# Eight gate dots on VectorE stated at other places of the first layer, and more of its sums pinned behind a product

## The chip, the core and the metric

The kernel runs on one core of a Trainium2 chip. The metric is the device time of one execution in microseconds; the time of a kernel is the median of its runs. An execution's time is a little longer than its span, which reaches from the first to the last instruction that the profiler recorded.

## The reference

Two layers over 256 tokens of width 2048, in f32. The first layer is a Mamba-2 mixer: one big input projection gives z, x, B, C and dt; x, B and C go through a causal convolution of width 4 and SiLU; then a state-space sum within one chunk of 256 tokens, in 8 groups of 8 heads; then a gate by SiLU(z), an RMS norm by group, and an output projection. The second layer is a dilated window attention. Each layer is wrapped in an adaptive norm: three vectors (shift, scale and gate) are products of SiLU(c) with a large matrix.

```python
def _adaln(c, w, b):
    mod = jax.nn.silu(c) @ w + b
    shift, scale, gate = jnp.split(mod, 3, axis=-1)
...
        h = x * (1.0 + scale) + shift
...
        x = _layer_norm(DEEPNORM_ALPHA * x + (1.0 + gate) * y, ln_g[layer], ln_b[layer])
```

The first layer's gate is needed only at the end of that layer. Its 2048 entries come from 16 dots, one for every 128 channels; the first eight of them are what the change moves.

The state-space sum of one group, as the kernel does it (one chunk, so the carried state drops out):

```python
        cb = jnp.einsum("blgn,bsgn->blsg", cc, bc)
        y_diag = jnp.einsum("blsgk,bsgkp->blgkp", cb[..., None] * decay, xc)
```

## The kernel before

**Weights in pieces.** All projections stream f32 weights from HBM in pieces of 128x1024 (tile raw, six buffers, loaded on SP's queue by load_piece, line 88). Each piece is split in two halves for the f32r matmuls: ScalarE copies the high half (whi, line 100) and VectorE makes the low half (wlo = raw - whi, line 102). There are four buffers of each half, so a half can be made while PE is up to four pieces behind it. A product then takes three matmuls for each pair of tiles: high by high, high by low, low by high. Lines 155 to 157 are the B and C products ("bc") and the second group's x product, lines 195 and 198 the other x products (cm_wide), and lines 238 to 240 the z products (tm_chunk, through tm_mults). A function called first_or takes a piece that begin_next has already split during the last piece of the product before.

**Order within an engine.** Each engine works through its own queue in order. That order is fixed when the program is built: a scheduler goes through the program and gives an engine, at each point, the oldest stated instruction that is ready by then, so that a younger one can be pulled in front of an older one that is not ready. `tc.issue_after(ins)` adds one fixed edge: what is stated in its block comes behind `ins` in the queue of their engine. It adds no other wait. In the texts, a pin is such an edge.

**The gate dots.** ada_load (line 315) loads one 1 MB slice of the modulation matrix into a tile araw (two buffers, SP's queue, line 317). ada_dot (line 320) is one VectorE instruction over 128x2048 elements with an accumulator (line 324), pinned behind `pin[0]`. queue (line 340) makes a list of jobs; each job loads the next slice and then states its own dot. The jobs are taken off by background (line 136), which every product calls once for each weight piece, with a rate (n, every): it adds n to a counter and states a job each time the counter reaches `every`. The rate is the variable R.

**The state-space part.** The loop over the groups (line 843) states for g = 0 to 6, in this order: for odd g the B and C products of the groups g+1 and g+2 with their convolutions; scores(g) (lines 751 and 752 on PE, then 754 and 755 on VectorE); the x product of group g+1; the normalisation of group g-1 (stage3, ScalarE, line 828); stage1(g), which makes the decay factors (ScalarE, lines 769 and 771) and multiplies them with the scores (VectorE, line 772, tile seg, two buffers); by_tokens(g), which turns x with eight transposes (line 784) and makes three scaled copies on VectorE (xd line 786, the skip term line 789, xo line 794); the convolution of group g+1's x (VectorE, line 399, three steps for each of four tiles); the z product of group g+1; and stage2(g), the sums. The groups are counted from 0 in the code, and from first to eighth in the texts: g = 1 is the second group. Part of several products has been done in an earlier phase, so they have fewer pieces: the z product of the third group has one piece, of the fourth group eight, of the fifth group four; the first B and C product in the loop has six pieces, the second (the fifth group's) two; the x product of the second group has six, all others eight.

The sums of a group are two f32 matmuls into po (line 806), which need xo, and 64 small matmuls into py (line 817), which need xd and seg; after them VectorE and ScalarE combine, gate and square them (lines 807 to 820) and take a reciprocal root in twelve tiny steps (lines 822 and 282 to 288). In the groups 0, 4 and 7 the py matmuls are pinned behind the last matmul of the newest z product (z_end, line 263). In the other groups they are free, as po is in all.

Before the change the eight jobs are queued at g = 1, with the rate (1, 10) and a counter that already stands above ten.

Of the kernel before, what the change touches and what calls it, by code (L numbers as in the profile page):

```python
# [49 lines left out]
def trunk(ctx, tc, xT, x, c, par, cst, bias, lnrow, ada, wdt, win, wxs, wout, wk, wv, wbin, wbout, out):  # L50
    nc = tc.nc
    V, S, T, PO = nc.vector, nc.scalar, nc.tensor, nc.gpsimd
# [287 lines left out]
    def queue(pool, cols):  # L340

        loaded = [ada_load(pool, *cols[0])]

        def step(i):
            raw = loaded.pop(0)
            if i + 1 < len(cols):
                loaded.append(ada_load(pool, *cols[i + 1]))
            ada_dot(*cols[i], raw)

        jobs.extend(lambda i=i: step(i) for i in range(len(cols)))  # L350
# [12 lines left out]
    with ExitStack() as cA:  # L363
# [15 lines left out]
        with ExitStack() as cS:  # L379
# [330 lines left out]
            aux = cS.enter_context(tc.tile_pool(name="aux", bufs=2, space=PSUM, reuse_waits="tile"))  # L710
            aux2 = cS.enter_context(tc.tile_pool(name="aux2", bufs=2, space=PSUM, reuse_waits="tile"))
            px = pe = cS.enter_context(tc.tile_pool(name="px", bufs=2, reuse_waits="tile"))
            R = (1, 10)


            scratch = wp1.tile([P, D], F32, name="araw")
# [41 lines left out]
            def stage1(g, cb):  # L758

                segs = []  # L760
                for w in range(2):
                    h0 = g * HPG + 4 * w
                    cbc = px.tile([P, 4, 2, P], F32, name="cbc")
                    nc.sync.dma_start(cbc, bass.AP(tensor=cumd.tensor, offset=cumd.offset + h0 * L,
                                                   ap=[[0, P], [L, 4], [P, 2], [1, P]]))
                    seg = px.tile([P, 4, 2, P], F32, name="seg")
                    for hh in range(4):
                        for b in range(2):
                            S.activation(seg[:, hh, b, :], cbc[:, hh, b, :], AF.Relu,
                                         bias=cumT[:, b, h0 + hh:h0 + hh + 1], scale=-1.0)  # L770
                    S.activation(seg, seg, AF.Exp, scale=-1.0)
                    V.tensor_tensor(seg.rearrange("p h b n -> p h (b n)"), seg.rearrange("p h b n -> p h (b n)"),
                                    cb[:, 0:2, :].rearrange("p b n -> p (b n)")[:, None, :].to_broadcast([P, 4, L]),
                                    op=ALU.mult)
                    segs.append(seg)
                return [segs, cb]
# [24 lines left out]
            def stage2(g, segs, cb, xd, xo):  # L801

                ss = sm.tile([P, 2], F32, name="ss")

                po = aux.tile([P, 512], F32, name="aux")
                T.matmul(po, cb[:, 2, :], xo, start=True, stop=True)
                V.tensor_tensor(xo.rearrange("p (h e) -> p h e", h=HPG), po.rearrange("p (h e) -> p h e", h=HPG),
                                dec[:, 1, g * HPG:(g + 1) * HPG, None].to_broadcast([P, HPG, 64]), op=ALU.mult)
                V.tensor_tensor(y[g][:, 1, :], xo, y[g][:, 1, :], op=ALU.add)
                behind = z_end[-1] if g in (0, 4, 7) else None  # L810
                for b in range(2):
                    py = aux2.tile([P, 512], F32, name="py")
                    for hh in range(HPG):
                        e_ = slice(64 * hh, 64 * hh + 64)
                        for t_ in (slice(0, 64), slice(64, 128)):
                            with tc.issue_after(behind.ins) if behind is not None else ExitStack():
                                T.matmul(py[t_, e_], segs[hh // 4][:, hh % 4, b, t_], xd[:, b, e_], start=True, stop=True)  # L817
                    V.tensor_tensor(y[g][:, b, :], py, y[g][:, b, :], op=ALU.add)
                    V.tensor_tensor(y[g][:, b, :], y[g][:, b, :], sz[g][:, b, :], op=ALU.mult)
                    S.activation(py, y[g][:, b, :], AF.Square, accum_out=ss[:, b:b + 1])  # L820
                ms = sm.tile([P, 2], F32, name="ms")
                V.tensor_scalar(ms, ss, 1.0 / 512, EPS, op0=ALU.mult, op1=ALU.add)
                return rsqrt(ms, "a")
# [17 lines left out]
            product("z", 0)  # L841
            rs = None
            for g in range(G - 1):
                if g == 1:
                    pin[0] = latest[-1].ins
                    queue(wp1, [(0, "gate", kt) for kt in range(KT // 2)])
                if g % 2 == 1:
                    product("bc", g + 1)
                cb = scores(g)
                convs = product("xs", g + 1)  # L850
                while chores:
                    chores.pop(0)()
                if rs is not None:
                    stage3(g - 1, rs)
                st1 = stage1(g, cb) + by_tokens(g)
                for convolve in convs:
                    if g < 2:
                        chores.append(lambda convolve=convolve: convolve(latest[-1].ins))
                    else:
                        convolve(None)  # L860
                if g < G - 2:
                    product("z", g + 1)
                rs = stage2(g, *st1)
# [613 lines left out]
```

## Time and profile before

| | |
|---|---|
| median of 3 runs | 1224.08 us (1222.66 to 1225.51) |
| the profiled execution's own time | 1222.2 us |
| its span | 1220.4 us |
| granted TensorE clock, mean | 1.000 |

Chunks of the profile are quoted as they stand. PE is TensorE's matmuls, PEld its weight loads, DVE is VectorE, ACT is ScalarE, SP is the engine that issues most DMAs. A row of the timeline gives start, duration, engine, line, operation, the tiles written and read, and the count; in brackets stands how long the engine had been idle before and what ended that. Instructions of one engine overlap at their ends, so the distance of two starts says more of a cost than the printed duration does: a low half (128x1024) takes 1.22 us by duration, and the next instruction starts 1.14 us after it. The stage table gives for each stretch its length and the busy time of each engine in it.

| where on PE (start, us) | what |
|---|---|
| 205.74 | second group's x product |
| 259.58 | third group's x product |
| 282.57 | third group's z product, one piece |
| 286.70 | second group's sums |
| 290.42 | fourth group's x product |
| 313.41 | fourth group's z product begins |
| 316.71 | third group's sums, inside it |
| 339.78 | fifth group's B and C product |
| 345.44 | fifth group's x product |
| 368.33 | fifth group's z product |
| 379.35 | fourth group's sums |
| 507.67 | eighth group's sums |

### The profile page before, as it was taken

What the parts mean: (1) busy time and instruction counts of PE and PEld (TensorE: products, weight loads), DVE (VectorE), ACT (ScalarE), POOL (GpSimd) and SP (SyncE); (2) the same over time, 40 slices, a digit from 0 to 9 for tenths busy, and PEclk for the clock granted to TensorE, in tenths of its full rate; (3) what the DMA queues carried; (4) which work ended last, traced back from release to release, by engine and by line L of the source; (5) the groups of instructions that cost most, each with busy time, mean ns of one, the idle gap of its engine ahead of it and who ended that gap; (6) DMA issues with size and microseconds to landing.
All of it is one profiled execution on the core that took longest, in us unless ns stands there. A gap on an engine that the chain in (4) does not pass through costs nothing.

```text
span 1220.4 us, 19064 instructions
## 1 busy us (share of the span) xinstructions
PE 1208.1 (99%) x7244; PEld 1040.6 (85%) x7244; DVE 1023.3 (84%) x1454; ACT 703.5 (58%) x1053; POOL 3.9 (0%) x8
## 2 busy tenths in 40 slices
PE   9999999999999999999999999999999999999998
PEld 8889998898888888788888888888888888888886
DVE  6989997899988999899778588888988975756886
ACT  4554567777967899764435455444435744444751
POOL 0000000000000000000000000000000000000001
PEclk9999999999999999999999999999999999999999
DMA  9999976787665556688988569989998685365673
GB/s 374 422 421 422 422 267 245 257 325 243 207 211 181 180 173 207 219 323 332 386 320 302 204 202 344 346 342 385 379 393 309 233 272 173 118 190 159 194 260 69
DMA packets 81372, 335.94 MB, mean 275 GB/s; under 512 B 9200, under 2 KB 9984, under 8 KB 68480
## 3 DMA queue, kind: packets, MB, share of 16 engines
q1 hardware_dynamic: 80496, 333.59, 74.9%
q0 software_dynamic: 576, 1.05, 0.6%
q8 instruction: 57, 0.93, 0.3%
q14 instruction: 35, 0.29, 0.1%
q10 hardware_dynamic: 208, 0.08, 0.0%
HBM read 331.45 MB, written 3.23 MB: 274 GB/s over the span
## 4 chain that ended last, share of the span: by engine, by line
PE 83%; DVE 9%; DMA 3%; ACT 3%; issue 2%; DVEq 0%; ACTq 0%; SPq 0%
PE acc L230 25%; PE acc L195 23%; PE acc L198 12%; PE acc L239 4%; DVE araw L324 4%; PE acc L240 4%; PE acc L238 3%; DVE wlo L102 3%; DMA raw<-in_win 2%; PE acc L157 2%; PE acc L155 2%; ACT whi L100 2%; PE acc L156 1%; PE py L817 1%; DMA araw<-in_ada 1%
## 5 line engine op out<-in xcount | busy, mean ns | idle before, releaser
L100 ACT ACTIVATE whi<-raw 128x1024 fp32r<-128x1024 f32 x389 | 408.2, 1057 | 331.0 <-PE acc L195 111.0
L102 DVE TENSOR_TENSOR wlo<-raw,whi 128x1024 fp32r<-128x1024 f32 x389 | 469.6, 1219 | 125.7 <-ACT whi L100 121.3
L195 PE MATMUL acc<-actT,whi 128*128 128x512 f32 x1280 | 401.2, 394 | 0.0
L198 PEld LDWEIGHTS acc<-actT,wlo 128*128 128x128 f32 x1280 | 239.6, 188 | 52.4
L198 PE MATMUL acc<-actT,wlo 128*128 128x256 f32 x1280 | 254.7, 280 | 0.0
L324 DVE SCALAR_TENSOR_TENSOR araw<-araw,cb__72 128x2048 f32<-128x2048 f32 x95 | 216.9, 2283 | 1.9 <-DMA araw<-in_ada 1.7
L195 PEld LDWEIGHTS acc<-actT,whi 128*128 128x128 f32 x1280 | 194.7, 188 | 0.6
L230 PE MATMUL acc<-whi,actT 128*128 128x512 f32 x560 | 144.0, 391 | 0.0
L230 PEld LDWEIGHTS acc<-whi,actT 128*128 128x128 f32 x560 | 104.1, 188 | 21.2
L239 PE MATMUL acc<-wlo,actT 128*128 128x512 f32 x272 | 106.7, 392 | 1.6 <-DVE wlo L102 1.6
L238 PE MATMUL acc<-whi,actT 128*128 128x512 f32 x272 | 104.7, 393 | 0.2 <-ACT sz L667 0.2
L157 PE MATMUL acc<-actT,wlo 128*128 128x256 f32 x372 | 101.8, 280 | 1.6 <-DVE wlo L102 1.6
L155 PE MATMUL acc<-actT,whi 128*128 128x256 f32 x372 | 103.1, 280 | 0.2
L156 PE MATMUL acc<-actT,whi 128*128 128x256 f32 x372 | 102.8, 278 | 0.0
L230 PE MATMUL acc<-wlo,actT 128*128 128x512 f32 x384 | 102.7, 389 | 0.0
L240 PE MATMUL acc<-whi,actT 128*128 128x512 f32 x256 | 99.9, 390 | 0.0
L230 PEld LDWEIGHTS acc<-wlo,actT 128*128 128x128 f32 x384 | 72.1, 188 | 15.0
L157 PEld LDWEIGHTS acc<-actT,wlo 128*128 128x128 f32 x372 | 68.9, 188 | 2.6 <-DVE wlo L102 2.6
L155 PEld LDWEIGHTS acc<-actT,whi 128*128 128x128 f32 x372 | 69.6, 188 | 1.5 <-ACT sz L667 0.5
L156 PEld LDWEIGHTS acc<-actT,whi 128*128 128x128 f32 x372 | 70.5, 189 | 0.3
L239 PEld LDWEIGHTS acc<-wlo,actT 128*128 128x128 f32 x272 | 51.1, 188 | 13.3 <-DVE wlo L102 3.1
L238 PEld LDWEIGHTS acc<-whi,actT 128*128 128x128 f32 x272 | 50.8, 188 | 10.6 <-ACT sz L667 0.6
(329 smaller groups left out, 1291.8 us busy)
## 6 DMA issues: line engine op xcount, KB each, us to landing
araw<-in_ada SPq DMA_DIRECT2D x96, 1024.0 KB, 7.5
raw<-in_win SPq DMA_DIRECT2D x109, 512.0 KB, 6.0
raw<-in_wout SPq DMA_DIRECT2D x64, 512.0 KB, 5.7
raw<-in_wbin SPq DMA_DIRECT2D x64, 512.0 KB, 4.3
raw<-in_wxs SPq DMA_DIRECT2D x48, 512.0 KB, 5.0
raw<-in_wv SPq DMA_DIRECT2D x48, 512.0 KB, 6.9
raw<-in_wk SPq DMA_DIRECT2D x48, 512.0 KB, 7.5
cbc<-cumd SPq DMA_DIRECT2D x16, 512.0 KB, 5.9
```

Source lines behind the costliest of these rows:

```text
L100: copied.append(S.activation(hi, raw, AF.Copy))
L102: latest.append(V.tensor_tensor(lo, raw, hi.bitcast(F32), op=ALU.subtract))
L155: T.matmul(o, hi[:, k, c_], ahi[:, kt, :], start=first, stop=False, skip_group_check=True)
L156: T.matmul(o, hi[:, k, c_], alo[:, kt, :], start=False, stop=False, skip_group_check=True)
L157: T.matmul(o, lo[:, k, c_], ahi[:, kt, :], start=False, stop=kt == k1 - 1, skip_group_check=True)
L195: T.matmul(ps[n], hi[:, k, n * P:n * P + P], both(kt), start=kt == 0, stop=False, skip_group_check=True)
L198: T.matmul(ps[n][:, 0, :], lo[:, k, n * P:n * P + P], high(kt), start=False, stop=kt == KT - 1, skip_group_check=True)
L230: T.matmul(ps[b], a_(kt)[:, b * P:b * P + P], w_[:, k, :], start=a_ is ahi and w_ is hi and kt == k0, stop=w_ is lo and kt == k1 - 1)
L238: T.matmul(o, h_, hi[:, k, :], start=kt == k0, stop=False, skip_group_check=part)
L239: T.matmul(o, h_, lo[:, k, :], start=False, stop=False, skip_group_check=part)
L240: end = T.matmul(o, l_, hi[:, k, :], start=False, stop=kt == k1 - 1, skip_group_check=part)
L324: return V.scalar_tensor_tensor(raw, raw, 1.0, cb_, op0=ALU.mult, op1=ALU.mult, accum_out=mod[layer][:, ct, j:j + 1])
```

## The change

The first eight gate dots are queued at g = 0 instead of g = 1, with the counter at zero. The rate is (1, 2) up to the convolution of g = 0, so that three are stated under the second group's x product (six pieces); it is (1, 1) in g = 3 up to the same place, so that the five others are stated under the fifth group's B and C product (two pieces) and the first three pieces of its x product, with a new pin behind the newest low half that is stated when g = 3 begins. Everywhere else the rate is (0, 99): none.

In stage2 the po matmuls too are pinned behind z_end where the py matmuls are, and the groups with the pin are 0, 2, 3, 4 and 7 instead of 0, 4 and 7.

```diff
-            R = (1, 10)
+            R = (0, 99)
...
+                behind = z_end[-1] if g in (0, 2, 3, 4, 7) else None
                 po = aux.tile([P, 512], F32, name="aux")
-                T.matmul(po, cb[:, 2, :], xo, start=True, stop=True)
+                with tc.issue_after(behind.ins) if behind is not None else ExitStack():
+                    T.matmul(po, cb[:, 2, :], xo, start=True, stop=True)
...
-                behind = z_end[-1] if g in (0, 4, 7) else None
...
             for g in range(G - 1):
-                if g == 1:
+                if g == 0:
                     pin[0] = latest[-1].ins
+                    state[0] = 0
                     queue(wp1, [(0, "gate", kt) for kt in range(KT // 2)])
+                R = (1, 2) if g == 0 else (1, 1) if g == 3 else (0, 99)
+                if g == 3:
+                    pin[0], state[0] = latest[-1].ins, 0
                 if g % 2 == 1:
                     product("bc", g + 1)
...
                 st1 = stage1(g, cb) + by_tokens(g)
+                R = (0, 99)
```

The second eight gate dots and everything behind the state-space part are stated as before.

## The prediction

> **What bounds the kernel now.** I read the page first, then the waits of PE in the state-space stretch, then that stretch by stages, then the few places where PE stands. The page:
>
> ```profile
> span 1220.4 us, 19064 instructions
> ...
> PE 1208.1 (99%) x7244; PEld 1040.6 (85%) x7244; DVE 1023.3 (84%) x1454; ACT 703.5 (58%) x1053; POOL 3.9 (0%) x8
> ```
>
> PE is busy for 1208.1 of 1220.4 us, so only what lets PE stand can be gained. The change touches the stretch from the second group's x product (about 205 us) to the last group's sums (about 512 us). This is all that PE waits for there, in the waits of PE (us in total, times, longest):
>
> ```profile
> PE aux L806 <- DVE xo L794: 1.1, 1, 1.1
> PE acc L239 <- DVE wlo L102: 1.0, 2, 0.5
> PE aux L882 <- DVE at L286: 0.7, 1, 0.7
> ```
>
> That is 2.8 us, or 0.23% of 1224.08: the most that any better order of VectorE's work can bring here. The same stretch by stages (length, then busy time and count of PE, PEld, DVE, ACT, POOL, clock, DMA share, GB/s):
>
> ```profile
> 205.00:223.00 18.00, 18.00 (x159) 17.91 (x157) 11.31 (x13) 17.09 (x29) 0.00 (x0) 1.00 0.80 287
> 223.00:240.00 17.00, 17.00 (x75) 13.66 (x74) 17.00 (x27) 10.38 (x16) 0.00 (x0) 1.00 0.67 226
> 240.00:290.00 50.00, 48.86 (x429) 43.87 (x428) 50.00 (x78) 36.78 (x63) 0.00 (x0) 1.00 0.88 312
> 290.00:313.00 23.00, 23.00 (x136) 20.28 (x136) 23.00 (x47) 22.77 (x43) 0.00 (x0) 1.00 0.62 201
> 313.00:340.00 27.00, 26.53 (x174) 21.65 (x173) 26.69 (x44) 23.23 (x43) 0.00 (x0) 1.00 0.64 219
> 340.00:368.00 28.00, 28.00 (x181) 25.36 (x180) 22.87 (x39) 18.66 (x29) 0.00 (x0) 1.00 0.61 196
> 368.00:383.00 15.00, 15.00 (x125) 12.21 (x123) 14.62 (x23) 9.15 (x17) 0.00 (x0) 1.00 0.50 162
> 383.00:418.00 35.00, 35.00 (x248) 30.07 (x247) 29.89 (x56) 28.74 (x52) 0.00 (x0) 1.00 0.56 186
> ```
>
> The rows from 223 to 313 show VectorE busy for 90.00 of 90.00 us, while PE loses 1.14 there. VectorE is full, and PE is hardly held up: a low half (wlo) is made up to four pieces ahead of its use.
>
> A rule reads this otherwise. The Trainium skill, Perfetto Trace Analysis, section Identifying the Most-Contended Engine, takes VectorE's occupancy as a fair measure of its limit and says to optimise the engine of highest occupancy first; by it VectorE, and not PE, would set the time of 240 to 313. I go by PE's own rows, and price the rule as a rival.
>
> **Where the dots run.** The dots are line 324; the view of that line from 200 to 345 and from 240 to 290 (count, shortest, median and longest in ns, first and last start):
>
> ```profile
> L324 DVE SCALAR_TENSOR_TENSOR araw<-araw,cb__72 x8: 2273/2276/2286, 236.8 to 337.4; 128x2048 f32<-128x2048 f32 x8
> ...
> L324 DVE SCALAR_TENSOR_TENSOR araw<-araw,cb__72 x5: 2273/2274/2278, 246.4 to 280.3; 128x2048 f32<-128x2048 f32 x5
> ```
>
> Each takes 2.28 us. The program states one in every ten weight pieces, over six groups, yet all run between 236.8 and 339.6, five of them between 246 and 283: the scheduler pulls them to wherever VectorE has nothing older to do. Statement places give a rank, pins alone give an order. What one costs, on VectorE and then on PE:
>
> ```profile
> 280.28 2.28 DVE L324 SCALAR_TENSOR_TENSOR araw<-araw,cb__72 128x2048 f32<-128x2048 f32 x1
> 282.49 0.07 DVE L324 DVE_READ_ACCUMULATOR araw<-araw,cb__72 128x1 f32 x1
> 282.49 1.21 DVE L102 TENSOR_TENSOR wlo<-raw,whi 128x1024 fp32r<-128x1024 f32 x1
> ...
> 285.29 0.67 DVE L789 TENSOR_TENSOR s<-aux,prm 128x512 f32<-128x512 f32 x1
> 285.88 0.67 DVE L794 TENSOR_TENSOR xo<-aux,dec 128x512 f32<-128x512 f32 x1
> ```
>
> ```profile
> 285.18 0.39 PE L240 MATMUL acc<-whi,actT 128*128 128x512 f32 x1
> 286.70 1.10 PE L806 MATMUL aux<-xo,cb 128*128 128x512 f32 x2 [1.14 <-DVE xo L794]
> ```
>
> The dot ends at 282.56, xo ends at 286.55, and PE, with the short z product done, stands for 1.14 us. Without this dot the chain behind it ends up to 2.28 us sooner.
>
> **The change, part by part.**
>
> *Second group's dots taken away.* With the five dots between 246 and 283 gone, 2.28 us (the dot at 280.28) leave the chain to xo and the wait of 1.14 goes: **-1.1 us**. Bounds: 0 (other vector work moves up into the dot's place) to -1.14. I take the whole, since 2.28 is twice 1.14. The next thing late there is the scores product behind it, which waits for nothing now.
>
> *Three dots under the second group's x product.* Between 205 and 223 VectorE has 18.00 - 11.31 = 6.7 us free, and three dots take 6.8. The cover is the four halves ahead of PE, and the xo of the first group, needed at 240 only. **0**; if the cover failed, at most one dot, 2.3 us. SP's queue is touched too: the third dot's load needs the first dot's buffer, and weight pieces queue behind it. How long SP can stand unharmed:
>
> ```profile
> 299.89 8.55 SPq L90 DMA_DIRECT2D raw<-in_win  x5
> 308.54 0.38 SPq L764 DMA_DIRECT2D cbc<-cumd  x1
> 321.07 2.96 SPq L90 DMA_DIRECT2D raw<-in_win  x3
> ...
> araw<-in_ada SPq DMA_DIRECT2D x96, 1024.0 KB, 7.5
> ```
>
> From 308.92 to 321.07 SP issued nothing and no matmul waited for a transfer, so 7.5 us of a load and the 2.3 of a dot are covered: 0. The moved pair of loads adds 2 MB to a stage at 287 GB/s, where 312 is carried later: 0. POOL has no part.
>
> *The third group's sums pinned behind its successor's z product.* The sums now run inside that product, because its second low half was not ready:
>
> ```profile
> 316.26 0.61 PE L238 MATMUL acc<-whi,actT 128*128 128x512 f32 x2
> 316.71 1.02 PE L806 MATMUL aux<-xo,cb 128*128 128x512 f32 x2
> ...
> 321.06 0.50 PE L239 MATMUL acc<-wlo,actT 128*128 128x512 f32 x1 [0.47 <-DVE wlo L102]
> ```
>
> ```profile
> 308.45 2.29 DVE L324 SCALAR_TENSOR_TENSOR araw<-araw,cb__72 128x2048 f32<-128x2048 f32 x1
> ...
> 310.73 1.22 DVE L772 TENSOR_TENSOR seg<-seg,cb 128x1024 f32<-128x1024 f32 x1
> ...
> 317.04 2.84 DVE L399 SCALAR_TENSOR_TENSOR cacc<-xs,prm,cacc 128x254 f32<-128x254 f32 x7
> 319.80 1.22 DVE L102 TENSOR_TENSOR wlo<-raw,whi 128x1024 fp32r<-128x1024 f32 x1
> ```
>
> Without the pin PE fills 316.71 to 320.59 (321.06 - 0.47) with the sums and the next scores, and waits 0.47. With it, the rest of the product (L239) stands first in PE's queue and wants that low half at 316.71. Behind it wait the whole z product and then the sums. The bounds of the new wait: 4.35 us (the half comes at 321.06 as now) and 0 (it is made before 313, where the dot at 308.45 leaves 2.28 free and the convolutions, L399, move up). If the chain moves by exactly one dot, 4.35 - 2.28 = 2.1 us are left; but five more dots are gone from in front of it, 11.4 us of vector work, so I put it near the low end: **+0.5, and -0.5** for the wait that is there now.
>
> *Five dots under the fifth group's products.* VectorE from 340 to 383 is busy 22.87 + 14.62 = 37.5 of 43 us. Five dots add 11.4. The pinned sums add their six vector steps (about 0.6 each by the starts 285.29 and 285.88) and a short root, some 5 us; and the two decay products (L772, 1.22 each) that must wait until the sums free their buffers, 2.4. That makes 56.3. Two dots can run earlier: their loads will have landed long before (nothing else uses the two buffers), and their pin is the low half of the first B and C piece, made four pieces ahead. The window also starts some 4 us sooner, at the end of the z product. So about 51.7 in 47: 5 us too much. It can be put off: the x convolution's second half (six of 0.4, by the seven in 2.84) is wanted a group later, and the xo of this stage, which the sums want, is early. I take **0**, with 0 and +5 as bounds: in 223 to 313 VectorE was full for 90 us, and PE lost 1.14. ScalarE takes over the decays of the fourth group too, with 28 - 18.66 = 9.3 us free in 340 to 368.
>
> *The other pins* (fourth group; and the first product of the sums in the first, fifth and eighth) put in writing what PE does now: 0.
>
> **Sum.** -1.1 - 0.5 + 0.5 = -1.1 us. The profiled execution took 1222.2 us (span 1220.4), which is 1.9 under the median of the runs, 1224.08. So 1221.1 for that execution, and **1223.0** for the median.
>
> **Rivals.**
>
> 1. *All waits of the stretch go* (2.8): 1221.3. For: all three hang on VectorE. Against: the last, at L882, belongs to the last group, 100 us behind the last dot. Chance 0.12.
> 2. *VectorE is the bound, as that rule has it*: the five dots out of 240 to 290 would give back 11.4 us, 1212.7. Against: PE is busy 48.86 of 50.00 there. Chance 0.02.
> 3. *Nothing is gained*: the free place is filled by other vector work of older rank, xo is as late as now, and the time is 1224.1. For: the scheduler already moves the dots far from where they are stated. Chance 0.16.
> 4. *Slower through the pin*: the low half stays as late as now, and PE stands 4.35 us in the z product of the fourth group: -1.1 - 0.5 + 4.35 = +2.8, 1226.9. The sum changes sign where that half comes at 318.3 (a wait of 1.6), and passes 2.4 us where it comes at 320.7 (4.0). For: the fill that the sums gave is lost, and ScalarE is busy for 22.77 of 23.00 before it. Against: the dot in front of it goes. Chance 0.12. The Trainium skill, TensorE: Matmul & The Clock Gate, section HAM oscillation — how this bites in real kernels, would add to it: PE gaps above some 3.4 us drop its clock to a half for a while, an estimated 1.7 us by that page; no row here shows this, every stage stands at 1.00 and no wait is longer than 1.14.
> 5. *Slower through the five dots*: the overload of 5 us reaches PE through late low halves in the x and z products: -1.6 + 5 = +3.4, 1227.5. Chance 0.08.
>
> **How the numbers follow.** About 0.2%, 2.4 us, is what a measurement of this kernel can tell from no change. My forecast has 0.50 and, with rival 3, stays within it: 0.66. Faster are rivals 1 and 2: 0.14. Slower are 4 and 5: 0.20. The range: below, rival 1 less half a microsecond of the scatter of the runs (1222.66 to 1225.51), 1220.8; above, to rival 4, 1226.8, which leaves out rival 5, the worse half of rival 4 and rival 2.
>
> **What would show it.** Right: three L324 between about 197 and 226, none from 230 to 325, five between 330 and 365; L806 of the second group directly behind L240 without a wait for xo; L806 of the third group behind the last L240 of the fourth group's z product, and no wait above 1 us for wlo in that product. Wrong: a wait for wlo of 2 us or more at L239 near 317 (rival 4), or several at L198 and L239 between 340 and 383 (rival 5); a wait for xo that stays (rival 3); waits for raw anywhere.

## The result, and the profile after

| | before | after |
|---|---|---|
| median of the runs | 1223.49 us (1222.60 to 1225.51, 6 runs) | 1229.91 us (1227.17 to 1231.86, 6 runs) |
| the profiled execution's own time | 1222.2 us | 1227.48 us |
| its span | 1220.4 us | 1225.7 us |

The ratio is 1.0049 [1.0036, 1.0062]: slower, by 6.4 us in the median and by 5.3 us between the two profiled executions. The prediction was 1223.0 in a range of 1220.8 to 1226.8, so the forecast had the wrong sign and the wrong size. The page of the kernel after:

```profile
span 1225.7 us, 19066 instructions
...
PE 1208.6 (99%) x7244; PEld 1039.6 (85%) x7244; DVE 1024.5 (84%) x1454; ACT 705.9 (58%) x1055; POOL 3.9 (0%) x8
```

The work is the same (PE 1208.6 against 1208.1), so the 5.3 us of span are standing time. The waits of PE from 200 to 520 us, in the kernel after (us in total, times, longest):

```profile
PE acc L239 <- DVE wlo L102: 4.0, 4, 2.2
PE acc L198 <- DVE wlo L102: 2.0, 2, 1.5
PE aux L888 <- DVE at L286: 0.7, 1, 0.7
```

They were 2.8 us and are 6.7. The wait for xo is gone, and waits for low halves have come in its place. The last line is that of before, L882, at its new line number; no wait for raw is among them. By stages (the columns are those of the prediction):

```profile
223.00:240.00 17.00, 16.43 (x77) 13.39 (x76) 15.99 (x26) 16.81 (x29) 0.00 (x0) 1.00 0.88 308
240.00:290.00 50.00, 50.00 (x435) 44.82 (x434) 41.50 (x70) 38.08 (x66) 0.00 (x0) 1.00 0.64 207
...
313.00:340.00 27.00, 24.77 (x145) 19.87 (x145) 23.67 (x31) 14.23 (x20) 0.00 (x0) 1.00 0.64 217
340.00:368.00 28.00, 25.99 (x193) 23.11 (x189) 28.00 (x51) 27.00 (x48) 0.00 (x0) 1.00 0.68 245
368.00:383.00 15.00, 14.27 (x69) 11.68 (x68) 14.57 (x25) 8.07 (x14) 0.00 (x0) 1.00 0.44 140
```

PE is now full from 240 to 290, where it lost 1.14, and loses 0.57, 2.23, 2.01 and 0.73 in the other rows. VectorE was full for the 50 us from 240 and has 8.5 free there now; the full stretch is 340 to 368.

Set side by side at the same matmul, the kernel after lies behind by 0.70 us at 200, 1.38 at 240, 0.09 at 290, 1.12 at 341, and 5.26 from the fourth group's sums to the end. The first 0.70 is ahead of all that the change does on PE: at that place the later profiles lie between -0.39 and +0.66, so it is scatter of single executions. The rest is four pieces, +0.7, -1.3, +1.0 and +4.1, and each belongs to a part of the change. At the fourth group's z product 0.57 us of work (the next scores) moved out and into the fifth group's x product, so the last two are rather +1.6 and +3.6.

**Gain, as predicted.** PE at the second group's sums, in the kernel after: the sums start in step behind the last matmul, with no wait.

```profile
286.56 0.39 PE L240 MATMUL acc<-whi,actT 128*128 128x512 f32 x1
286.79 1.07 PE L808 MATMUL aux<-xo,cb 128*128 128x512 f32 x2
```

**Loss in the fourth group's z product.** PE, then VectorE, in the kernel after:

```profile
319.02 0.61 PE L238 MATMUL acc<-whi,actT 128*128 128x512 f32 x2
321.87 0.50 PE L239 MATMUL acc<-wlo,actT 128*128 128x512 f32 x1 [2.23 <-DVE wlo L102]
```

```profile
313.05 1.23 DVE L102 TENSOR_TENSOR wlo<-raw,whi 128x1024 fp32r<-128x1024 f32 x1
314.19 0.75 DVE L208 TENSOR_TENSOR xs<-acc,xs 128x256 f32<-128x256 f32 x2
...
317.85 2.84 DVE L399 SCALAR_TENSOR_TENSOR cacc<-xs,prm,cacc 128x253 f32<-128x253 f32 x7
320.61 3.48 DVE L102 TENSOR_TENSOR wlo<-raw,whi 128x1024 fp32r<-128x1024 f32 x3
```

The second piece's low half is made at 313.05, so PE gets one piece further than before. The third stands behind the step that takes over the x product's last sums (L208), five scaled copies and seven convolution steps: a chain that begins when PE ends the x product. Dots taken away far ahead of it do not move it. The low half at the end of this chain starts at 320.61, and at 319.80 before: even without the dot at 308.45 in front, the chain has not moved up. What shortens the wait is that the second piece's low half now stands in the dot's place, so that PE has 12 matmuls (2.7 us) more to do first.

**Loss in the fifth group.** VectorE, then PE, in the kernel after:

```profile
344.75 1.22 DVE L102 TENSOR_TENSOR wlo<-raw,whi 128x1024 fp32r<-128x1024 f32 x1
345.88 2.28 DVE L324 SCALAR_TENSOR_TENSOR araw<-araw,cb__72 128x2048 f32<-128x2048 f32 x1
...
353.82 1.22 DVE L102 TENSOR_TENSOR wlo<-raw,whi 128x1024 fp32r<-128x1024 f32 x1
...
355.75 2.28 DVE L324 SCALAR_TENSOR_TENSOR araw<-araw,cb__72 128x2048 f32<-128x2048 f32 x1
...
358.35 1.22 DVE L102 TENSOR_TENSOR wlo<-raw,whi 128x1024 fp32r<-128x1024 f32 x1
```

```profile
357.54 0.62 PE L195 MATMUL acc<-actT,whi 128*128 128x512 f32 x2
359.62 0.51 PE L198 MATMUL acc<-actT,wlo 128*128 128x256 f32 x2 [1.46 <-DVE wlo L102]
```

Between 344.75 and 353.82 no low half is begun; the last dot then stands for 2.2 us in front of the one that PE waits for, with one convolution step (0.4) in between.

**Loss in the second group's z product** (0.57). SP's queue in the kernel before, then after: the write of the running sums (L745), the dots' loads (L317), the decay rows (L764).

```profile
202.85 0.50 SPq L745 DMA_DIRECT2D cumd<-araw  x1
206.27 0.81 SPq L764 DMA_DIRECT2D cbc<-cumd  x2
```

```profile
207.37 0.50 SPq L745 DMA_DIRECT2D cumd<-araw  x1
208.50 0.33 SPq L90 DMA_DIRECT2D raw<-in_win  x1
211.03 0.80 SPq L317 DMA_DIRECT2D araw<-in_ada  x2
211.88 1.59 SPq L764 DMA_DIRECT2D cbc<-cumd  x2
```

The first dot, at 199.98, stands inside VectorE's chain from softplus to the running sums, so that these are written 4.5 us later: 2.2 us are the dot, and the rest is mostly two low halves that now come in between. Two 1 MB loads now stand directly ahead of the decay rows. The median time from issue to landing, in the view of transfers issued from 200 to 215, for the kernel before and then after:

```profile
cbc<-cumd SPq DMA_DIRECT2D x2, 512.0 KB, 4.4
```

```profile
cbc<-cumd SPq DMA_DIRECT2D x2, 512.0 KB, 9.8
```

The first rows land at 210.2 before and at 221.3 after. The decays, and the low halves that stand behind them on VectorE, follow. Of these 11 us only 0.7 reach PE here.

### The profile page after: what moved, and what is told of

The parts are those of the page before. It is cut to its first block, busy times and chain, and to the rows that moved or that the text cites. A ratio compares the mean times of both kernels' runs of the same rounds, so it can differ in the third digit from the quotient of the medians.

```text
span 1225.7 us, 19066 instructions
## 1 busy us (share of the span) xinstructions
PE 1208.6 (99%) x7244; PEld 1039.6 (85%) x7244; DVE 1024.5 (84%) x1454; ACT 705.9 (58%) x1055; POOL 3.9 (0%) x8
## 4 chain that ended last, share of the span: by engine, by line
PE 81%; DVE 10%; DMA 4%; ACT 4%; issue 2%; DVEq 0%; ACTq 0%
PE acc L230 25%; PE acc L195 23%; PE acc L198 12%; DVE araw L324 4%; DMA raw<-in_win 3%; PE acc L239 3%; PE acc L240 3%; PE acc L238 3%; DVE wlo L102 3%; ACT whi L100 2%; PE acc L157 1%; PE acc L155 1%; PE acc L156 1%; PE py L818 1%; DVE cacc L399 1%
## 5 line engine op out<-in xcount | busy, mean ns | idle before, releaser
L198 PEld LDWEIGHTS acc<-actT,wlo 128*128 128x128 f32 x1280 | 239.3, 188 | 54.9 <-DVE wlo L102 2.7
L198 PE MATMUL acc<-actT,wlo 128*128 128x256 f32 x1280 | 254.8, 280 | 2.0 <-DVE wlo L102 2.0
```

What stands on the lines that cost most here:

```text
L198: T.matmul(ps[n][:, 0, :], lo[:, k, n * P:n * P + P], high(kt), start=False, stop=kt == KT - 1, skip_group_check=True)
```

## The experiments

Times are medians. The kernels were run in four groups, each with the kernel before beside it (1223.20, 1223.05, 1222.85 and 1223.26 us), and the ratios are to that. The letters in the expectations hold for their group only. In the first group, theory A was two places (the pin takes PE's fill from the fourth group's z product, and five dots with the put-off sums crowd the fifth group), rival B the dots alone, rival C the pin alone.

### One part alone

**The dots alone**: the sums free as before.

```diff
-                behind = z_end[-1] if g in (0, 2, 3, 4, 7) else None
...
-                with tc.issue_after(behind.ins) if behind is not None else ExitStack():
-                    T.matmul(po, cb[:, 2, :], xo, start=True, stop=True)
+                T.matmul(po, cb[:, 2, :], xo, start=True, stop=True)
...
+                behind = z_end[-1] if g in (0, 4, 7) else None
```

> The dots are moved as in the change, the sums are left as before (no pin on the third and fourth group's sums, none on po). Theory A (two places: the pin takes away what PE had to fill a late low half in the fourth group's z product, and the five dots together with the put-off vector work of those sums crowd the fifth group): the third group's sums run inside the fourth group's z product again, the wait for wlo there is at most 0.6 us, VectorE between 340 and 383 has some 7 us less to do, and the waits for wlo there fall from 2.7 us to under 1. The second group's wait for xo (1.14) stays away. Time 1222.5 to 1225. Theory B (the five dots alone): the waits at L198 and L239 between 350 and 380 stay near 2.7, time 1226 to 1229. Theory C (the pin alone): 1222 to 1223, all waits of the stretch near 1.5.

Measured: 1226.56 us, 1.0025 [1.0016, 1.0034]. The number lies in rival B's range, but not for B's reason: PE stands for 1.47 us in the fifth group, not 2.7, and some 2.2 us are lost in the second group's z product, which no theory named.

**The pins alone**: the dots as before.

```diff
+                behind = z_end[-1] if g in (0, 2, 3, 4, 7) else None
...
-                T.matmul(po, cb[:, 2, :], xo, start=True, stop=True)
+                with tc.issue_after(behind.ins) if behind is not None else ExitStack():
+                    T.matmul(po, cb[:, 2, :], xo, start=True, stop=True)
...
-                behind = z_end[-1] if g in (0, 4, 7) else None
```

> The pins of the change on the dots of before. Theory A: the z product of the fourth group waits 2.2 to 4.4 us for wlo, since a dot still runs at 308; the second group's wait of 1.14 is there as before; no wait above 0.5 between 340 and 383, since five dots less are there. Time 1225.5 to 1228. Theory B (the dots alone): as before, 1223 to 1224. Theory C (the pin alone): all of the loss, 1229 to 1230.

Measured: 1228.44 us, 1.0043 [1.0029, 1.0056], between the ranges of A and C. PE in the fourth group's z product, in this kernel:

```profile
319.97 0.61 PE L238 MATMUL acc<-whi,actT 128*128 128x512 f32 x2
324.78 0.80 PE L239 MATMUL acc<-wlo,actT 128*128 128x512 f32 x1 [4.20 <-DVE wlo L102]
325.37 0.63 PE L240 MATMUL acc<-whi,actT 128*128 128x512 f32 x1
325.80 0.63 PE L239 MATMUL acc<-wlo,actT 128*128 128x512 f32 x1
```

The wait is 4.20, and the matmuls behind it start 0.43 us apart, where 0.227 is usual: the granted clock is halved. The row of that stretch in the stage table, for this kernel:

```profile
320.00:330.00 10.00, 5.80 (x16) 4.34 (x15) 10.00 (x15) 3.74 (x7) 0.00 (x0) 0.66 0.37 114
```

A mean clock of 0.66 over 10 us is 6.8 us at one half. This profile is of the slowest run (1231.73 us); in it the second group's z product loses 3.5 us too, behind decay rows that landed 2 us late.

**The third group's sums free**: all of the change but that pin.

```diff
-                behind = z_end[-1] if g in (0, 2, 3, 4, 7) else None
+                behind = z_end[-1] if g in (0, 3, 4, 7) else None
```

> The change without one of its pins: the third group's sums are free, the others are pinned. Theory A: within 1 us of the run with no new pins at all, 1222.5 to 1225, since the other pins state what PE does anyway. If the fourth group's pin or the ones on po cost something, it is slower than that run by it. Theory B: 1226 to 1229.

Measured: 1226.45 us, 1.0031 [1.0020, 1.0042]; no wait above 0.5 in the fourth group's z product. So about 3.5 us of the 6.4 go with this one pin, and what is left is what the dots alone cost (1226.56), though both lie above the time that theory A gave. B and C each account for a part only. Alone they cost 3.4 and 5.2 us, together 6.4: with the dots as before, one of them still runs in front of the chain, and the pin's wait is 4.20 instead of 2.23.

**Five dots left out**: only the first three are queued; the other five entries are left at zero.

```diff
-                    queue(wp1, [(0, "gate", kt) for kt in range(KT // 2)])
+                    queue(wp1, [(0, "gate", kt) for kt in range(3)])
+                    V.memset(mod[0][:, 3:8, 2:3], 0.0)
```

> The change with the last five of the eight dots left out (their entries of the gate are set to zero): three dots under the second group's x product, and all pins. Theory A: the wait of 2.2 us in the fourth group's z product stays, since the five dots ran behind it, and the waits between 350 and 380 (2.7 us) shrink to under 0.6. Time 1225.5 to 1227.5. Theory B (the dots alone): 1222 to 1223. Theory C (the pin alone): 1229 to 1230. Where the granted clock was under 1.000 in executions of the change, it should be 1.000 here if only the sum of waits near 355 lowers it, and not if the one wait of 2.2 does.

Measured: 1231.67 us, 1.0066 [1.0053, 1.0078]: slower than with the dots, against every expectation. As theory A had it, the wait of 2.2 us in the fourth group's z product stays, and in the fifth group the waits go. The stage from 340 to 372 in this kernel, and then in the kernel after:

```profile
340.00:372.00 32.00, 32.00 (x243) 28.07 (x242) 25.40 (x50) 27.48 (x49) 0.00 (x0) 1.00 0.60 176
```

```profile
340.00:372.00 32.00, 29.99 (x217) 26.61 (x213) 32.00 (x58) 28.20 (x49) 0.00 (x0) 1.00 0.68 245
```

Without the five dots PE is never idle there, although the put-off sums are still there. With the dots the put-off sums do add: PE stands 1.47 us in the fifth group with the dots alone, and 2.74 in the kernel after. But in the second group's z product PE now waits 3.99 us for a low half and goes on at half the clock: the program's fixed order came out otherwise, with the splits of two pieces behind the decays, which wait for the late rows. A shorter program is not the same program less some work, so its time says nothing of the five dots' price.

### The clock, and where the early dots cost

**First dots behind the running sums.** In the kernel after, the first three dots are pinned behind the copy that ends that chain (line 744).

```diff
-            V.tensor_copy(cumr, pr)
+            cum_end = V.tensor_copy(cumr, pr)
...
-                    pin[0] = latest[-1].ins
+                    pin[0] = cum_end.ins
```

> The changed kernel with one edge altered: the first three dots are pinned behind the copy of the running sums (line 744) instead of the newest low half, so that none can run inside the softplus and running-sum chain. Theory A (three separate losses; the first is the dot at 199.98, which sends the running sums 4.5 us later to their transfer, so that the decay rows land at 221 instead of 210): the rows land near 211 again, the wait of 0.6 in the second group's z product goes, the waits in the fourth group's z product (2.2) and in the fifth group (2.7) stay; 1229.0, 0.5 to 1.2 us less than the changed kernel. Rival (any dot under this product costs the same, through its 1 MB load or VectorE's time): the rows land near 220 all the same and the time is 1229.9.

Measured: 1233.28 us, 1.0083 [1.0069, 1.0097], 3.4 more than the kernel after. Both theories were wrong. SP's queue in this kernel:

```profile
202.47 0.50 SPq L745 DMA_DIRECT2D cumd<-araw  x1
204.67 1.78 SPq L317 DMA_DIRECT2D araw<-in_ada  x2
206.51 0.91 SPq L764 DMA_DIRECT2D cbc<-cumd  x2
213.02 0.33 SPq L317 DMA_DIRECT2D araw<-in_ada  x1
```

The running sums are on time again, but a dot that ends at once frees its buffer at once, so two 1 MB loads now slip in ahead of the decay rows, and SP stands from 207.5 to 213.0 for the next free buffer, with the weight pieces behind it. The wait in the second group's z product is 2.56.

**The same with the sums free as before**: the same two edits, on the kernel with the dots alone.

> The sums as before (free in the third and fourth group), the dots as in the change, with the first three pinned behind the copy of the running sums. Theory A: of the 3.9 us that the kernel with the dots alone lay behind in its profile, 2.2 came in the second group's z product and go; the wait for xo stays away (-1.3); the five dots' wait at L198 (1.5) stays: 1224.3. Rival (the five dots cost all of it): 1226.6, as with the dots alone.

Measured: 1226.66 us, 1.0030 [1.0019, 1.0042]: no better than with the dots alone. The rival had the number, but not the reason: the second group's z product still loses some 2.1 us, with the first rows landing at 215.5 behind two loads.

**The five dots later**: as the one before, with the five stated one in every four pieces from g = 4 on.

```diff
-                R = (1, 2) if g == 0 else (1, 1) if g == 3 else (0, 99)
-                if g == 3:
+                R = (1, 2) if g == 0 else (1, 4) if g > 3 else (0, 99)
+                if g > 3:
```

> As the kernel before it in this list, but the five dots are stated one in every four pieces from the fifth group's stage on (g = 4 and later), where VectorE has about 5 us free in 35, instead of one a piece in g = 3. Theory A: the wait at L198 in the fifth group goes and no other of that size comes: 1222.5, 0.7 less than before. Rival (VectorE is as full there, the dots wait for nothing and PE does): 1224 to 1226, with new waits for wlo between 390 and 500.

Measured: 1225.68 us, 1.0022 [1.0013, 1.0031]. The wait at L198 in the fifth group goes, and new ones, up to 0.94 us, stand between 430 and 500: the rival, though the longest is for VectorE's copy of the scores (line 755) and not for a low half.

**PE's wait filled.** On the kernel with the pins alone, eight constant f32 matmuls in front of the second piece of the fourth group's z product.

```diff
+            last_end[0] = end
...
+                def fill(q):
+                    if q == 1:
+                        d = aux2.tile([P, 512], F32, name="py")
+                        for _ in range(8):
+                            with tc.issue_after(last_end[0].ins):
+                                T.matmul(d, ident, cb_[:, 0:512], start=True, stop=True)
...
-                    product("z", g + 1)
+                    product("z", g + 1, fill if g == 2 else None)
```

> The kernel with the pins alone, and eight f32 matmuls of 128x512 on constants, read by nothing, put on PE in front of the second piece of the fourth group's z product, where PE stands for 4.2 us; the orders of all engines are else the same. Theory C (the wait lowers the granted clock, half of it for up to 6.8 us, and that is part of the price): the wait is filled, the clock stays at 1.000 there, the 512-wide matmuls behind it start every 0.227 us instead of 0.427, and the time is 1226.3, about 2 less than with the pins alone. Rival (the late low half is the whole price): 1228.4, unchanged.

Measured: 1229.76 us, 1.0055 [1.0042, 1.0067]. The clock stayed whole, but the eight took 6.46 us and outlasted the wait. So it says nothing of what the lowered clock costs: the fill was too long.

**The same with five.**

```diff
-                        for _ in range(8):
+                        for _ in range(5):
```

> The fill again with five matmuls in place of eight: the eight took 6.46 us and ended 1.7 us behind the low half that PE waits for (321.87), so that their own length hid what the clock gave. Five take 4.0 and end before that half is made. Theory C (the wait lowers the clock, and that is part of the price of the pin): the clock stays at 1.000 in the fourth group's z product and the time is 1226.5 to 1227.4, 1 to 2 us less than with the pins alone (1228.44). Rival (the late low half is the whole price): 1228.4.

Measured: 1226.99 us, 1.0032 [1.0019, 1.0044], against 1.0043 without the fill. It lies 4.1 us behind the kernel before of its own group, the pins alone 5.2: about 1.1 us of the pin's price is the clock, by medians whose intervals overlap. The two profiles are plainer: from the start of the fourth group's z product to the fifth group's, PE falls behind the kernel before by another 5.7 us with the pins alone, and by 3.5 with the fill, so 2.2 us there are the clock. The stage in the profile of this kernel:

```profile
320.00:330.00 10.00, 10.00 (x42) 7.53 (x42) 9.89 (x11) 3.29 (x5) 0.00 (x0) 1.00 0.68 211
```

**The dots' loads on POOL's queue**, in the kernel after:

```diff
+    own = [False]
...
-        nc.sync.dma_start(raw, ada[layer, KIND.index(kind), ct])
+        (nc.gpsimd if own[0] else nc.sync).dma_start(raw, ada[layer, KIND.index(kind), ct])
...
+                    own[0] = True
                     queue(wp1, [(0, "gate", kt) for kt in range(KT // 2)])
...
+            own[0] = False
```

> The changed kernel, with the loads of the eight dots issued on POOL's queue instead of SP's. Theory A2 (under the second group's x product the dots' loads hold up SP's queue: the decay rows and five weight pieces stand behind them): in the second group's z product the wait goes; as the dot at 199.98 still delays the running sums, the decay rows land some 5 us later than before, not 11; 1229.2, 0.7 less than the changed kernel. Rival (it is VectorE's time, or the loads' share of the transfer engines, whatever the queue): unchanged, 1229.9.

Measured: 1235.64 us, 1.0102 [1.0087, 1.0116]. What A2 said of the rows came true: the dot delays the running sums, nothing stands ahead of the rows, they take 4.7 us (median) and the first lands at 215.3, 5.1 later than before. The time did not follow: PE is 6.0 us behind at the end of the second group's z product.

**Both**: these loads on POOL's queue and the dots behind the running sums.

> Both at once: the dots' loads on POOL's queue, and the first three dots pinned behind the copy of the running sums (line 744). Theory A2 (the pin alone lost because the dots then held their buffers and SP stood for 5.5 us between two of their loads, with the weight pieces behind it): now the wait in the second group's z product is gone, the decay rows land near 211, and the losses of the fourth and fifth group (2.2 and 2.8) stay; 1228.5 to 1229, against 1233.28 with the pin alone. Rival (the dots' place on VectorE is what costs): 1233, as with the pin alone.

Measured: 1233.99 us, 1.0091 [1.0077, 1.0105]. Theory A2 falls as an account of the time: another queue does not help. Weight pieces issued beside these loads, from 208 to 214, take 9.1 to 14.1 us in the two kernels, and 4.5 to 5.4 in the kernel before. In the first of the two a dot also stands on VectorE and waits for its load, with the low halves behind it. VectorE in that kernel:

```profile
220.84 2.29 DVE L326 SCALAR_TENSOR_TENSOR araw<-araw,cb__72 128x2048 f32<-128x2048 f32 x1 [7.10 <-DMA araw<-in_ada]
...
223.06 1.22 DVE L102 TENSOR_TENSOR wlo<-raw,whi 128x1024 fp32r<-128x1024 f32 x1
```

**Five and three**: the kernel before, with five dots in g = 1 and the last three pinned into g = 3.

```diff
                 if g == 1:
                     pin[0] = latest[-1].ins
                     queue(wp1, [(0, "gate", kt) for kt in range(KT // 2)])
+                R = (1, 3) if g in (1, 3) else (0, 99)
+                if g in (1, 3):
+                    pin[0], state[0] = latest[-1].ins, 0
```

> The kernel before with one difference: the dots one in every three pieces, five of them in g = 1, the last three pinned into g = 3, so that none runs between 262 and 325 us; the sums and SP's order else as before. Theory A (the wait for xo comes from the sixth dot at 280.28, the wait for wlo at 321 from the one at 308.45, and two or three dots fit into the 5.1 us that VectorE has free between 340 and 368): both waits go, no new one over 0.5 comes; 1221.7, 1.5 less than before. Rival (the fifth group has no room for three dots): a wait for wlo of 1 to 2 us at L198 there, 1223.2 to 1224.

Measured: 1222.43 us, 1.0000 [0.9991, 1.0009]. The waits of PE from 200 to 520 in this kernel:

```profile
PE acc L239 <- DVE wlo L102: 1.3, 2, 0.8
PE aux L885 <- DVE at L286: 0.7, 1, 0.7
```

Both waits that were named (xo, and the half at 321) are gone and none came in the fifth group, so the change's aim can be had in the profile without its pins. Of the 1.6 us, 0.8 is lost at once in the second group's z product, where the decay rows landed at 211.1 in this execution and at 210.2 in that of before; the median gain of 0.4 is less than can be told from none.

### One half of a dot at a time

**Two loads less**, in the kernel with the dots alone: the second and third dot work on the first one's slice again.

```diff
+            if cols[0] == (0, "gate", 0) and i < 2:
+                loaded.append(raw)
-            if i + 1 < len(cols):
+            elif i + 1 < len(cols):
```

> The kernel with the dots alone, but the second and third dot work on the first dot's slice again, so that two of the three 1 MB loads under the second group's x product are left out (two gate entries are left out with them). Theory T (the loads fill the transfer engines: 343 GB/s and a share of 0.93 from 196 to 223 against 298 and 0.83 before, so the decay rows and weight pieces land late): the rows land near 215 instead of 222 and 225, the 2.2 us lost in the second group's z product fall under 1; 1225.3. Rival V (the dots' time on VectorE): 1226.6, as with the dots alone.

Measured: 1227.93 us, 1.0040 [1.0027, 1.0052]. (The 343 GB/s of the expectation is the row of the kernel with the first dots behind the running sums; with the dots alone it is 320, at a share of 0.89.) SP's queue and the transfers issued from 200 to 215 in this kernel:

```profile
206.72 0.51 SPq L747 DMA_DIRECT2D cumd<-araw  x1
...
209.43 0.33 SPq L317 DMA_DIRECT2D araw<-in_ada  x1
```

```profile
cbc<-cumd SPq DMA_DIRECT2D x2, 512.0 KB, 8.8
```

**The loads alone**: a copy of one column in place of each of the three dots.

```diff
-            ada_dot(*cols[i], raw)
+            if cols[0] == (0, "gate", 0) and i < 3:
+                V.tensor_copy(mod[0][:, i, 2:3], raw[:, 0:1])
+            else:
+                ada_dot(*cols[i], raw)
```

> The complement: all three loads stay, and the first three dots are left out (a copy of one column stands in for each, so three gate entries are left out). Theory T: the rows land some 5 us later than in the kernel before, and 1 to 2 of the 2.2 us stay lost in the second group's z product; 1226. Rival V: VectorE has no dots there, nothing is late in that product, and the time is 1224.4.

Measured: 1227.79 us, 1.0040 [1.0026, 1.0053]. SP's queue, the transfers issued from 200 to 215, and VectorE in this kernel:

```profile
202.87 0.51 SPq L748 DMA_DIRECT2D cumd<-araw  x1
...
206.42 2.79 SPq L317 DMA_DIRECT2D araw<-in_ada  x2
209.27 0.90 SPq L767 DMA_DIRECT2D cbc<-cumd  x2
```

```profile
cbc<-cumd SPq DMA_DIRECT2D x2, 512.0 KB, 9.1
```

```profile
223.12 1.23 DVE L775 TENSOR_TENSOR seg<-seg,cb 128x1024 f32<-128x1024 f32 x1 [6.65 <-ACT seg L774]
```

The running sums are as early as in the kernel before (202.87 and 202.85), no dot is on VectorE, and still the first rows land at 217.9, 7.7 us later than before: SP issues them 3.0 us later, as it has to wait for a free buffer before the second load ahead of them, and they take 9.1 us instead of 4.4. VectorE stands idle for 6.65 us, waiting for decays. So the loads alone suffice; rival V falls as an only cause.

With two loads less, the dot inside the chain makes the running sums late (written at 206.7), one load still stands ahead, and the rows land at 218.2. So theory T, by which it takes all three loads, falls too; but one load is left in this kernel, so it does not show the dot alone. The kernel with the loads on POOL's queue does: no load ahead of the rows, the dot in the chain, and they land 5.1 us late. Either half is enough to make the rows late, and together they give 11. PE loses some 3.9 us in the second group's z product with two loads less and 3.6 with the loads alone, more than the 2.2 with both: both act through one thing, the landing of the decay rows, and its price depends on the order.

What that lateness costs PE depends on how many low halves the fixed order has put ahead of the decays: 0.6 us in the kernel after, 4.0 with the five dots left out, with the rows landing at 221.3 and 219.0. With the order of before, the landings and the wait behind them move together: 210.2 and none, 210.8 and 0.71 (fill of five), 211.1 and 0.52 (fill of eight), 211.1 and 0.80 (five and three), 212.4 and 1.85 (pins alone). PE itself is early or late by up to 0.25 us in these executions; measured from its place, the rows are 0.8, 0.7, 0.9 and 2.0 us late, and the order fits too. The kernel before has hardly any slack at this place.

## Why the prediction was wrong, point by point

- **The wait for xo goes, -1.1: right.** It went, and the stretch gained 1.3.
- **Three dots under the second group's x product, 0: wrong.** The step counted VectorE's free time (6.7 against 6.8 us, which was there) and then called the loads covered, from a stretch where SP may stand unharmed, 308.92 to 321.07, and from a rate of 312 GB/s carried elsewhere. The loads moved to 202 to 212, where the decay rows pass, and these rows had hardly any slack: with the order of before, each microsecond of their landing is nearly a microsecond of PE. The changed order let 11 us of lateness through for 0.7 us in the profile after, and for 2.2 in the profile of the dots alone. The step also missed that a dot can be pulled into the chain to the running sums.
- **The third group's pin, +0.5 with -0.5 for the old wait: the right mechanism, mis-sized.** The bounds were 4.35 if the half stays as late, and 2.1 if one dot goes from in front. Measured were 4.20 with the dots as before and 2.23 with the dot at 308.45 gone. That 2.23 is so near to 2.1 is luck: the chain did not move up by a dot (the half starts at 320.61, before at 319.80), PE got one more piece instead. The step that failed is the choice near the low end, "but five more dots are gone from in front of it": the chain ahead of that half begins when PE ends the x product, so dots before 290 cannot move it. Rival 4 named a late half and gave it 0.12.
- **The clock.** Rival 4 left it as a rule without a row. The Trainium skill, TensorE: Matmul & The Clock Gate, section HAM oscillation — how this bites in real kernels, speaks of gaps above some 3.4 us; here a halved clock is shown behind 4.20 (0.66 in the row above). The 1.7 us that rival 4 put down by that page are near what one spell cost here, 1.6 us, and it also falls behind shorter waits; both stand in the last section. The 2.4 us by which the median lies above the profiled execution go with it: the two runs with a mean clock of 1.000 took 1227.17 and 1227.48, the four below it 1229.29 to 1231.86.
- **Five dots in the fifth group, 0 within 0 and +5: wrong, inside its bounds.** It cost some 3.6 us. The overload of 5 us had been worked out, and was then waved off with the 90 us in which VectorE was full at little cost. Being full says nothing of slack: in those 90 us the low halves were ahead of PE; here the dots, pinned into a few pieces, come in front of them. Rival 5 named it (its sum, -1.6 + 5, leaves out the +0.5 that the forecast has for the pin).
- **The other pins, 0:** no wait of PE in the profile after stands at them. The VectorE work of the fourth group's later sums is harmless by itself, as the kernel with the five dots left out shows (PE 32.00 of 32.00), but with the five dots there it seems to add to the standing (2.74 against 1.47, by two profiles).

On the profiled execution the sum is 0.7 (scatter) + 0.7 - 1.3 + 1.6 + 3.6 = 5.3, in place of -1.1. Rivals 4 and 5 both came true, each at less than its price in this execution (a wait of 2.23 for 4.35, and 3.6 for 5); taken as separate cases with chances of 0.12 and 0.08, they were never added.

What stays open: why the order of steps in the second group's z product comes out with few or many low halves ahead of the decays (it is fixed when the program is built), and how much of the 6.4 us in the median is clock. The fill gives 1.1 us for the pin alone in the medians and 2.2 in the profiles, and one spell of lowered clock behind the wait of 2.2 costs about 1.6 us (below).

## What to carry to other kernels

When a step moves, look up the slack of its transfers at the place they move to, not where some happens to be free, and follow what the stated order will put behind them: a 1 MB load that costs nothing at one place can make a transfer late that a chain waits for at another. When two bounds are far apart, ask which instruction starts the chain; work taken away ahead of that point gives nothing. And where two rivals touch different stages, they can both come true, so their prices belong in one sum.

## What the runs showed of the hardware

- A halved granted clock followed waits of PE of about 2 us. With the pins alone it followed one of 1.85 at 233.7 (a mean of 0.90 from 223 to 240). The wait of 2.2 in the fourth group's z product stands in five profiles: with the five dots left out and with the first dots behind the running sums, a stretch of some 3.3 us with starts 0.43 us apart followed; in the kernel after, and in the two with the loads on POOL's queue, the starts stayed at 0.23. So the length of the wait does not decide it alone, and one profile can miss a loss that most executions have. The stage in the kernel after, then in the kernel with the first dots behind the running sums:

```profile
316.00:334.00 18.00, 15.77 (x70) 12.72 (x69) 14.67 (x19) 8.03 (x10) 0.00 (x0) 1.00 0.61 206
```

```profile
316.00:334.00 18.00, 15.78 (x63) 12.50 (x62) 14.18 (x21) 8.39 (x12) 0.00 (x0) 0.91 0.53 173
```

PE is busy as long in both, but a mean of 0.91 over 18 us is 3.2 us at one half, so 1.6 us less is done.
- The two 512 KB transfers of the decay rows took 4.4 to 5.0 us (median) from issue to landing with no 1 MB load issued directly ahead of them, 7.3 and 8.8 with one on the same queue, and 8.3 to 10.1 with two.
